# A fused transformer block on one core: norm sums by a product with ones, a later second key group, two y tiles in the weight ring, and last products by token tile

## The chip, the cores and the metric

The kernel runs on one core of a Trainium2 chip. It is one launch. The metric is the device time of that launch in microseconds (us), median of several runs. Five engines work side by side, each on its own queue of instructions: TensorE (PE, matrix products into PSUM banks), VectorE (DVE), ScalarE (ACT), GpSimd (POOL) and SyncE (SP, which issues most DMA transfers). PEld is TensorE's loading of the stationary operand.

## What is computed

A decoder block for 512 tokens of width 2048 in fp32, one sequence: a root-mean-square norm, one wide projection, eight attention heads of kind A (compressed, selected and windowed attention, mixed by gates), sixteen narrow heads of kind B (a band of 128 tokens with a sink), each widened with a SiLU gate, then an output projection, the residual sum and a final norm.

```python
for l in range(DEPTH):
    h = _rmsnorm(x, norm_g[l])
    proj = h @ w_in[l]
    (qa, kca, vca, ksa, vsa, kwa, vwa, za, ga,
     qb, kb, vb, zb) = jnp.split(proj, offsets, axis=-1)
    ...
    o_a = gates[..., 0:1] * o_cmp + gates[..., 1:2] * o_sel + gates[..., 2:3] * o_win
    y_a = o_a.reshape(B, S, WIDTH_A) * jax.nn.silu(za)
    qb = _rope(_heads(qb, N_HEADS_B, HEAD_DIM_B)).reshape(B, S, N_KV_B, GROUP_B, HEAD_DIM_B)
    o_b = _banded_attention(qb, _rope(_heads(kb, N_KV_B, HEAD_DIM_B)), _heads(vb, N_KV_B, HEAD_DIM_B),
                            WIN_B, sink=sinks[l].reshape(N_KV_B, GROUP_B))
    y_b = o_b.reshape(B, S, WIDTH_B) * jax.nn.silu(zb)
    x = x + jnp.concatenate([y_a, y_b], axis=-1) @ w_out[l]
return _rmsnorm(x, final_g)
```

## The kernel before

**Split products.** Each fp32 operand is held as a high half in a rounded fp32 type (ScalarE copies it) and a low half (VectorE subtracts the high half from the original). A product is three matmuls, high by high, high by low, low by high (`mm3`, lines 90 to 92). So each weight that arrives by DMA in a `raw` tile takes a ScalarE pass (`whi`, line 68) and a VectorE pass (`wlo`, line 69), both of 128x1024; `wp` is a ring of three such buffers.

**The norm.** The tokens' squares are summed into `sqa` (128 x 512: tokens along the free axis). Four products with a column of ones (line 159) give the sums with tokens on partitions, `rstd` is one over their root, and four copies and four transposes (165, 166) spread it over the partitions as `rstdb` (167). `cosA` and `sinA` are scaled by `rstdb` (170, 171) before the first rope.

**The projections** use 512 columns a matmul and two PSUM banks, `pj`, that rotate. `q_rope` is three VectorE passes (95 to 97) that read the bank and a GpSimd add (349). A head's attention transposes probabilities (443, 578), splits them (`ph` on ScalarE, 377; `pl` on VectorE, 378), multiplies them with the values (450 to 452, 465, 467) and finishes into a y tile `yp` (364).

**From A to B.** After the last A head, key projection `wkb` is roped into `kb1`, query projection `wz[16]` follows, and `build_kv` makes for each of two key groups a doubled copy `kd` (four VectorE copies, 506), its high half `KBH` (507) and low half `KBL` (508), and then the values' halves `VB`. Eight steps over pairs of B heads follow, each with a projection for the next query and one for its gate `zr` (340).

**The output projection** is split by 512 output columns, n = 0 to 3. For n = 0, eight units of weights of two y tiles each go into four banks (`split_y`, 625 and 626, makes the halves of all 16 y tiles). For n = 1 to 3 the products of pairs are combined with fewer multiplications: y combinations named p, u, q (`combos`, 638 to 641), weights that are sums of quarters, and seven products by name (p, 22, u, 21, w, 12, q) whose banks are then added and subtracted. A sum of weight quarters is made by `summed`: SP loads one quarter, GpSimd issues a DMA that adds another to it (762). `ch` holds a running sum on VectorE (769); `u4` is the weight of product 12 (sum `s2`), `u5` of u, `u6` of q, and `s1` belongs to w. The halves of a weight are made by `split_to` (629, 630).

**The end.** `square` (655) sums squares of a row's columns on ScalarE, `pre_norm` (665) adds them, `final` takes the root and its reciprocal (670, 671), scales four pieces of 512 columns (674 on ScalarE, 676 and 678 on VectorE) and writes each by a DMA of 256 KB (675 on ScalarE's queue, 677 and 679 on SP's). The last products in order are u, 21, w, 12, q, of which only u and q are made token tile by token tile.

**What sets the order.** The program is written in one sequence, but a scheduler of the framework puts each engine's instructions in an order of its own by estimated readiness, and sets the waits. A pool's buffers rotate: a tile waits until the earlier tile in its buffer is no longer read. `issue_after` holds an instruction behind a named one. On each engine, instructions run in the order that results.

Of the kernel before, what the change touches and what calls it, by code (L numbers as in the profile page):

```python
# [10 lines left out]
F32 = mybir.dt.float32  # L11
# [22 lines left out]
def hybrid_block(ctx, tc, xT, xtm, w0, w1s, w2s, wz, wkb, wo0, wos, cw1, cw2, cpos, rope, tabs, sinks, gT, fg, out):  # L34
# [53 lines left out]

    def mm3(ps, ah, al, bh, bl, first, last, go_on=False):
        pe.matmul(ps, ah, bh, start=first, stop=False, skip_group_check=go_on)  # L90
        pe.matmul(ps, ah, bl, start=False, stop=False, skip_group_check=go_on)  # L91
        pe.matmul(ps, al, bh, start=False, stop=last, skip_group_check=go_on)  # L92

    def rope_mul(t1, t2, ps, cos, sin):
        dve.tensor_tensor(out=t1, in0=ps, in1=cos, op=ALU.mult)
        dve.tensor_tensor(out=t2[0:64], in0=ps[64:128], in1=sin[64:128], op=ALU.mult)
        dve.tensor_tensor(out=t2[64:128], in0=ps[0:64], in1=sin[0:64], op=ALU.mult)  # L97
        return t1, t2
# [38 lines left out]
    ones = s0.tile([P, 1], F32, name="ones")  # L137
# [29 lines left out]
    act.activation(rstdb, psr, AF.Copy)  # L167
# [177 lines left out]
    def q_rope(ps, cos, sin):  # L345
        t1 = wk.tile([P, S], F32, name="t1", tag="t1")
# [152 lines left out]
    def build_kv(t1):  # L499
        for g in range(2):  # L500
            kd = wk.tile([P, S], F32, name="kd", tag="t1")
            for half in range(2):
                for v in range(2):
                    d = half * 64 + v * 32
                    r = half * 64 + g * 32
                    dve.tensor_copy(kd[d:d + 32], t1[r:r + 32])
            act.activation(KBH[:, g, :], kd, AF.Copy)
            pool.tensor_tensor(out=KBL[:, g, :], in0=kd, in1=KBH[:, g, :].bitcast(F32), op=ALU.subtract)
# [113 lines left out]
    rs2 = so.tile([P, NQ, 2], F32, name="rs2")  # L622

# [9 lines left out]
    ops = {}  # L633

    def combos(m):
        f1, f2 = 2 * m, 2 * m + 1
        a11, a21, a12, a22 = yt[f1][:, H0], yt[f1][:, H1], yt[f2][:, H0], yt[f2][:, H1]
        dve.tensor_tensor(out=a21, in0=a11, in1=a21, op=ALU.subtract)
        dve.tensor_tensor(out=a11, in0=a11, in1=a12, op=ALU.subtract)
        dve.tensor_tensor(out=a12, in0=a12, in1=a21, op=ALU.subtract)  # L640
        dve.tensor_tensor(out=a22, in0=a22, in1=a12, op=ALU.subtract)
        for nm, src in (("p", a11), ("u", a12), ("q", a21)):
            hi = cmb.tile([P, 256], F32R, name=f"{nm}h{m}")
            lo = cmb.tile([P, 256], F32R, name=f"{nm}l{m}")
# [22 lines left out]
    def final(t, part):  # L667
# [5 lines left out]
        for n in range(2):  # L673
            act.activation(v[n], v[n], AF.Copy, scale=r)
            nc.scalar.dma_start(out[:, t, n * 512:n * 512 + 512], v[n])
        dve.tensor_scalar(v[2], v[2], r, None, op0=ALU.mult)
        nc.sync.dma_start(out[:, t, 1024:1536], v[2])
        dve.scalar_tensor_tensor(out=v[3], in0=v[3], scalar=r, in1=fgt[1][:, 512:1024], op0=ALU.mult, op1=ALU.mult)
# [37 lines left out]
    def halves(raw):  # L716
        hi = wp.tile([P, 1024], F32R, name="whi", tag="whi")
        lo = wp.tile([P, 1024], F32R, name="wlo", tag="wlo")
        split_to(hi, lo, raw)
        return hi, lo  # L720

    fgt = []
    for n in range(1, 4):
        xs.append([late(2 * n - 2 + T) for T in range(2)])
        src = wos[n - 1]
        ba, bb, bx, bc = [b.rearrange("p (t c) -> p t c", c=256) for b in banks(n)]
# [57 lines left out]
        product(ba, [halves(load(raw(), 0, g)) for g in range(2)], "p", True)  # L784
        e3 = scratch()
        act.activation(e3, ba, AF.Copy)
# [38 lines left out]
        else:  # L825
            by = psf1.tile([P, S], F32, name="oa", tag="oa").rearrange("p (t c) -> p t c", c=256)
            bxt = [bx, by]
# [19 lines left out]
            product(bc, [halves(c) for c in s1], "w", True)  # L847
            s2 = summed(raw, 0, 2)
            for t in range(2):
                times_g(2, t)  # L850
            plus(xa[1], xa[1], bc)
            u4 = [halves(c) for c in s2]
            u6 = [halves(c) for c in ch]
            for t in range(2, 4):
                square(ssq[:, t, 4:5], xs[3][1][:, t - 2, :])
                pre_norm(t, 4)
                final(t, ssq[:, t, 4:5])
            product(ba, u4, "12", False)
            plus(xb[0], xb[0], ba, ALU.subtract)
            plus(xa[0], xa[0], ba)  # L860
            for t in range(2):
                square(ssq[:, t, 4:5], xa[0][:, t, :])
                pre_norm(t, 5)
# [78 lines left out]
```

## Time and profile before

| what | us |
|---|---|
| median of three runs (850.31 to 850.93) | 850.83 |
| the profiled execution | 850.5 |
| its span on the core | 848.7 |
| VectorE busy | 597.1 |
| ScalarE busy | 404.7 |
| GpSimd busy | 94.1 |

The page gives each engine's busy time and its share of the span. A timeline row gives start, duration, engine, line, operation, output and input by their names in the program, shape, and in square brackets the idle time of that engine before it and what ended it. A list of waits gives the instruction, what released it, total, number and longest. In this kernel 128x512 matmuls are recorded at about 0.40 us each, but overlap: their starts are nearer to each other than that.

### The profile page before, as it was taken

The page shows a single profiled execution, that of the slowest core. Times are in us where ns is not written, and L with a number is a line of the kernel's source. Part 1 is how long each engine was busy: PE and PEld are TensorE (multiplying, and loading weights), DVE is VectorE, ACT ScalarE, POOL GpSimd, SP SyncE. Part 2 cuts the span into 40 slices and gives each one's busy share as a digit, 9 for nine tenths or more (in the row PEclk, how much of TensorE's full clock was granted, in tenths as well). Part 3 has the DMA queues.
Part 4 walks back from the last instruction along what each step waited for, and adds up shares of the span by engine and source line. Part 5 has one row for each costly group of instructions (what it writes and reads, how often), then busy time and mean ns, then how long its engine had stood idle before and what let it go on. Part 6 is the DMA issues. An engine that isn't in the chain of part 4 may idle for free.

```text
span 848.7 us, 12742 instructions
## 1 busy us (share of the span) xinstructions
PE 833.0 (98%) x4776; PEld 727.2 (86%) x4776; DVE 597.1 (70%) x1244; ACT 404.7 (48%) x845; POOL 94.1 (11%) x71
## 2 busy tenths in 40 slices
PE   9999999999999999999999999999999999999994
PEld 7787899988888888888888788888888788999994
DVE  7829574645676765665767698777677799768785
ACT  6724345443554443544443456444543747444436
POOL 4500002011110110110111210111011000000010
PEclk9999999999999999999999999999999999999998
DMA  9642275542221212121221212221223137895975
GB/s 326 202 128 75 78 228 179 170 124 75 75 75 50 65 60 75 51 75 61 90 75 51 86 64 75 76 90 59 75 75 99 51 85 262 215 292 127 283 176 198
DMA packets 33773, 101.40 MB, mean 119 GB/s; under 512 B 4016, under 2 KB 4016, under 8 KB 33712
## 3 DMA queue, kind: packets, MB, share of 16 engines
q1 hardware_dynamic: 30400, 90.90, 33.0%
q0 software_dynamic: 2016, 7.34, 4.9%
q10 hardware_dynamic: 1296, 2.36, 0.8%
q8 instruction: 37, 0.61, 0.3%
q14 instruction: 24, 0.20, 0.1%
HBM read 96.39 MB, written 4.19 MB: 119 GB/s over the span
## 4 chain that ended last, share of the span: by engine, by line
PE 90%; DMA 3%; DVE 2%; ACT 2%; issue 1%; POOL 0%; ACTq 0%; SPq 0%; DVEq 0%; POOLq 0%
PE pj L91 17%; PE pj L92 17%; PE pj L90 17%; PE oa L90 4%; PE oa L92 4%; PE oa L91 4%; PE bank L92 4%; PE bank L90 4%; PE bank L91 4%; PE sp L408 3%; PE tp L443 2%; DMA xr<-xT 1%; PE tp L578 1%; DMA raw<-wos 1%; PE op L452 1%
## 5 line engine op out<-in xcount | busy, mean ns | idle before, releaser
L90 PE MATMUL pj<-xh,whi 128*128 128x512 f32 x560 | 222.8, 398 | 1.2 <-DVE t L97 1.2
L91 PE MATMUL pj<-xl,whi 128*128 128x512 f32 x560 | 222.2, 397 | 0.0
L92 PE MATMUL pj<-xh,wlo 128*128 128x512 f32 x560 | 221.9, 397 | 0.0
L69 DVE TENSOR_TENSOR wlo<-raw,whi 128x1024 fp32r<-128x1024 f32 (+2 forms) x130 | 149.8, 1158 | 75.1 <-ACT whi L68 71.7
L68 ACT ACTIVATE whi<-raw 128x1024 fp32r<-128x1024 f32 (+2 forms) x129 | 124.9, 971 | 153.0 <-PE pj L91 65.0
L90 PEld LDWEIGHTS pj<-xh,whi 128*128 128x128 f32 x560 | 105.4, 188 | 23.1 <-DVE t L97 1.4
L91 PEld LDWEIGHTS pj<-xl,whi 128*128 128x128 f32 x560 | 105.4, 188 | 22.4 <-issue 1.0
L92 PEld LDWEIGHTS pj<-xh,wlo 128*128 128x128 f32 x560 | 105.4, 188 | 22.4
L349 POOL TENSOR_TENSOR t<-t,t 128x512 f32<-128x512 f32 x17 | 35.9, 2114 | 388.8 <-DVE t L97 370.1
L90 PE MATMUL oa<-whi,yh 128*128 128x256 f32 (+1 forms) x208 | 61.9, 299 | 0.6 <-ACT yh L625 0.6
L91 PE MATMUL oa<-wlo,yh 128*128 128x256 f32 (+1 forms) x208 | 62.2, 299 | 0.0
L92 PE MATMUL oa<-whi,yl 128*128 128x256 f32 (+1 forms) x208 | 61.6, 299 | 0.0
L378 DVE TENSOR_TENSOR pl<-tp,ph 128x512 fp32r<-128x512 f32 x56 | 37.8, 685 | 33.3 <-ACT ph L377 33.2
L377 ACT ACTIVATE ph<-tp 128x512 fp32r<-128x512 f32 x56 | 32.5, 595 | 57.0 <-PE tp L443 44.6
L90 PEld LDWEIGHTS oa<-whi,yh 128*128 128x128 f32 x208 | 39.1, 188 | 2.1 <-ACT yh L625 0.8
L92 PEld LDWEIGHTS oa<-whi,yl 128*128 128x128 f32 x208 | 39.2, 188 | 1.4
L91 PEld LDWEIGHTS oa<-wlo,yh 128*128 128x128 f32 x208 | 39.2, 188 | 1.3
L91 PE MATMUL bank<-wlo,xh 128*128 128x256 f32 (+1 forms) x128 | 40.1, 315 | 0.0
L92 PE MATMUL bank<-whi,xl 128*128 128x256 f32 (+1 forms) x128 | 39.9, 314 | 0.0
L557 ACT ACTIVATE ttb<-ttb,mnb 128x256 f32<-128x256 f32 (+1 forms) x64 | 30.1, 471 | 18.2 <-DVE mnb L550 17.6
L90 PE MATMUL bank<-xh,whi 128*128 128x512 f32 x96 | 37.2, 398 | 0.4 <-ACT whi L68 0.4
L91 PE MATMUL bank<-xl,whi 128*128 128x512 f32 x96 | 37.4, 394 | 0.0
(277 smaller groups left out, 1718.3 us busy)
## 6 DMA issues: line engine op xcount, KB each, us to landing
raw<-wz SPq DMA_DIRECT2D x64, 512.0 KB, 3.7
raw<-cw SPq DMA_DIRECT2D x16, 512.0 KB, 3.7
raw<-wos SPq DMA_DIRECT2D x14, 512.0 KB, 4.6
rw<-wos SPq DMA_DIRECT2D x12, 512.0 KB, 5.0
xr<-xT SPq DMA_DIRECT2D x16, 256.0 KB, 5.3
raw<-w SPq DMA_DIRECT2D x8, 512.0 KB, 4.4
raw<-wo SPq DMA_DIRECT2D x8, 512.0 KB, 3.7
raw<-w SPq DMA_DIRECT2D x15, 256.0 KB, 4.6
```

The source lines that it names most:

```text
L68: act.activation(hi[:, :width], raw[:, :width], AF.Copy)
L69: last["lo"] = dve.tensor_tensor(out=lo[:, :width], in0=raw[:, :width], in1=hi[:, :width].bitcast(F32), op=ALU.subtract).ins
L90: pe.matmul(ps, ah, bh, start=first, stop=False, skip_group_check=go_on)
L91: pe.matmul(ps, ah, bl, start=False, stop=False, skip_group_check=go_on)
L92: pe.matmul(ps, al, bh, start=False, stop=last, skip_group_check=go_on)
L349: pool.tensor_tensor(out=t1, in0=t1, in1=t2, op=ALU.add)
L377: act.activation(ph, tp, AF.Copy)
L378: dve.tensor_tensor(out=pl, in0=tp, in1=ph.bitcast(F32), op=ALU.subtract)
L408: pe.matmul(sp[:, a:b], qq[:, qs], kk[g][:, ko:ko + b - a], start=pi == 0, stop=pi == 2)
L443: pe.transpose(tp[:, e * 256 + i * P:e * 256 + i * P + P], views[2 * i + w][2][:, kt * P:(kt + 1) * P], ident)
L452: pe.matmul(oc, VL[:, kt, w, vs], ph[:, es], start=False, stop=False)
L557: act.activation(tv, tv, AF.Exp, bias=mn[:, e, v:v + 1], scale=-1.0, accum_out=dn[:, e, v:v + 1])
```

## The change

The change has five parts.

1. The norm's sums come from one product of a 128x128 tile of ones with `sqa`, whose result is already spread over the partitions; the root and the reciprocal are taken on 128x512. The column sums for `rstd` stay. Copies and transposes go.
2. `build_kv` becomes `build_k` for one group and `build_v`. The second group is built after the query projection of the next heads. `kd` and `kb1` now lie in the pool `wb`, and the copies are held behind the last rope issued.
3. The halves of y tiles 0 and 1 for the first unit (n = 0) are made in a buffer of the weight ring (`ey`), ahead of the point at which the pool of the y halves opens. `split_y` still makes all y halves.
4. In the last stage (n = 3) the products p, w, 12 and q are made by token tile, each tile in a bank of its own, and sums, squares and `final` follow tile by tile in the order 2, 3, 0, 1. The halves of `s2` go into the buffers of the p combinations, free after product p. All pieces but one of the output leave on SP's queue. `behind` holds a tile's sums behind the previous tile's last scaling.
5. A root of one column is taken at the start of the output projection, so that the table of that function is loaded there.

```diff
-    ones = s0.tile([P, 1], F32, name="ones")
+    ones = s0.tile([P, P], F32, name="ones")
...
     psr = bank(6)
+    pe.matmul(psr, ones, sqa, start=True, stop=True)
+    psc = bank(7)
     for t in range(NQ):
-        pe.matmul(psr[:, t:t + 1], sqa[:, t * P:(t + 1) * P], ones, start=True, stop=True)
-    act.activation(rstd, psr[:, 0:NQ], AF.Sqrt, bias=eps, scale=1.0 / D)
+        pe.matmul(psc[:, t:t + 1], sqa[:, t * P:(t + 1) * P], ones[:, 0:1], start=True, stop=True)
+    act.activation(rstdb, psr, AF.Sqrt, bias=eps, scale=1.0 / D)
+    act.activation(rstd, psc[:, 0:NQ], AF.Sqrt, bias=eps, scale=1.0 / D)
+    dve.reciprocal(rstdb, rstdb)
     dve.reciprocal(rstd, rstd)
-    psr = bank(7)
-    for t in range(NQ):
-        rb = s0b.tile([P, P], F32, name="rb", tag="rb")
-        dve.tensor_copy(rb, rstd[:, t:t + 1].to_broadcast([P, P]))
-        pe.transpose(psr[:, t * P:(t + 1) * P], rb, ident)
-    act.activation(rstdb, psr, AF.Copy)
...
-    def build_kv(t1):
-        for g in range(2):
-            kd = wk.tile([P, S], F32, name="kd", tag="t1")
-            for half in range(2):
-                for v in range(2):
-                    d = half * 64 + v * 32
-                    r = half * 64 + g * 32
+    def build_k(t1, g):
+        kd = wb.tile([P, S], F32, name="kd", tag="kd")
+        for half in range(2):
+            for v in range(2):
+                d = half * 64 + v * 32
+                r = half * 64 + g * 32
+                with tc.issue_after(last["rope"]):
                     dve.tensor_copy(kd[d:d + 32], t1[r:r + 32])
...
-    kb1 = q_rope(proj(wkb), cosB, sinB)
+    kb1 = q_rope(proj(wkb), cosB, sinB, wb.tile([P, S], F32, name="kb1"))
     q2 = qb_evac(proj(wz[16]))
-    build_kv(kb1)
+    build_k(kb1, 0)
+    build_v()
     for i in range(8):
         tts = softmax_b(i, q2)
         if i < 7:
             q2 = qb_evac(proj(wz[17 + i]))
+        if i == 0:
+            build_k(kb1, 1)
         st = z_evac(proj(wz[24 + i]))
         if i == 7:
+            ey = [wp.tile([P, 1024], F32R, name=nm, tag=nm) for nm in ("whi", "wlo")]
+            y01 = ypair[0].rearrange("p a b -> p (a b)")
+            act.activation(ey[0], y01, AF.Copy)
+            dve.tensor_tensor(out=ey[1], in0=y01, in1=ey[0].bitcast(F32), op=ALU.subtract)
...
+    act.activation(rs2[:, 0, 0:1], ssq[:, 0, 0:1], AF.Sqrt)
...
+    pq = [cmb.tile([P, 8, 256], F32R, name=f"p{e}", tag=f"p{e}") for e in "hl"]
...
+    @contextmanager
+    def behind(t):
+        if t == 2:
+            yield
+        else:
+            with tc.issue_after(last["fin_act"]), tc.issue_after(last["fin_dve"]):
+                yield
...
-                mm3(acc[t], yh[f][:, ts], yl[f][:, ts], hi[:, ws], lo[:, ws], f == 0, f == 15)
+                if f < 2:
+                    ah, al = [y[:, f * S:(f + 1) * S] for y in ey]
+                else:
+                    ah, al = yh[f], yl[f]
+                mm3(acc[t], ah[:, ts], al[:, ts], hi[:, ws], lo[:, ws], f == 0, f == 15)
...
-            product(bc, [halves(c) for c in s1], "w", True)
+            u1 = [halves(c) for c in s1]
             s2 = summed(raw, 0, 2)
...
-            u4 = [halves(c) for c in s2]
+            p4 = [cmb.tile([P, 8, 256], F32R, name=f"p{e}", tag=f"p{e}").rearrange("p a b -> p (a b)") for e in "hl"]
+            u4 = [halves(s2[g], [p[:, g * 1024:g * 1024 + 1024] for p in p4]) for g in range(2)]
             u6 = [halves(c) for c in ch]
...
+            for t in range(2):
+                with tc.issue_after(recent["mm"]):
+                    product(bct[t], u1, "w", True, (t,))
+                with behind(2 + t):
+                    plus(xa[1][:, t, :], xa[1][:, t, :], bct[t][:, t, :])
+                    square(ssq[:, 2 + t, 4:5], xs[3][1][:, t, :])
+                final(2 + t, ssq[:, 2 + t, 4:5])
             for t in range(2):
-                product(bxt[t], u6, "q", False, (t,))
-                v = xb[0][:, t, :]
-                plus(v, v, bxt[t][:, t, :])
-                square(ssq[:, t, 5:6], v)
+                with tc.issue_after(recent["mm"]):
+                    product(bat[t], u4, "12", False, (t,))
+                va, vb = xa[0][:, t, :], xb[0][:, t, :]
+                with behind(t):
+                    plus(va, va, bat[t][:, t, :])
+                    plus(vb, vb, bat[t][:, t, :], ALU.subtract)
+                    square(ssq[:, t, 4:5], va)
+                    pre_norm(t, 5)
+                with tc.issue_after(recent["mm"]):
+                    product(bxt[t], u6, "q", False, (t,))
+                plus(vb, vb, bxt[t][:, t, :])
+                square(ssq[:, t, 5:6], vb)
                 final(t, ssq[:, t, 5:6])
```

More of the change, by code (lines that the diff above doesn't have):

```diff
@@ L1 @@
-from contextlib import ExitStack
+from contextlib import ExitStack, contextmanager
 import numpy as np
@@ L91, in mm3 @@
         pe.matmul(ps, ah, bl, start=False, stop=False, skip_group_check=go_on)
-        pe.matmul(ps, al, bh, start=False, stop=last, skip_group_check=go_on)
+        recent["mm"] = pe.matmul(ps, al, bh, start=False, stop=last, skip_group_check=go_on).ins
     def rope_mul(t1, t2, ps, cos, sin):
@@ L96, in rope_mul @@
         dve.tensor_tensor(out=t2[0:64], in0=ps[64:128], in1=sin[64:128], op=ALU.mult)
-        dve.tensor_tensor(out=t2[64:128], in0=ps[0:64], in1=sin[0:64], op=ALU.mult)
+        last["rope"] = dve.tensor_tensor(out=t2[64:128], in0=ps[0:64], in1=sin[0:64], op=ALU.mult).ins
         return t1, t2
@@ L714, in late, with halves, as_pair @@
         return yp.tile([P, 2, S], F32, name=f"late{k}", tag=f"yp{k}")
-    def halves(raw):
-        hi = wp.tile([P, 1024], F32R, name="whi", tag="whi")
-        lo = wp.tile([P, 1024], F32R, name="wlo", tag="wlo")
+    def halves(raw, to=None):
+        hi, lo = to or [wp.tile([P, 1024], F32R, name=nm, tag=nm) for nm in ("whi", "wlo")]
         split_to(hi, lo, raw)
         return hi, lo
+    def as_pair(b):
+        return b.rearrange("p (t c) -> p t c", c=256)
     fgt = []
@@ L725, in hybrid_block @@
         src = wos[n - 1]
-        ba, bb, bx, bc = [b.rearrange("p (t c) -> p t c", c=256) for b in banks(n)]
+        ba, bb, bx, bc = [as_pair(b) for b in banks(n)]
         xa = [x[:, :, H0] for x in xs[n]]
@@ L782, in plus @@
             dve.tensor_tensor(out=out, in0=a, in1=b, op=op)
-        product(ba, [halves(load(raw(), 0, g)) for g in range(2)], "p", True)
+        u3 = [halves(load(raw(), 0, g)) for g in range(2)]
         e3 = scratch()
-        act.activation(e3, ba, AF.Copy)
+        if n < 3:
+            product(ba, u3, "p", True)
+            act.activation(e3, ba, AF.Copy)
+        else:
+            bat = [ba, as_pair(psf1.tile([P, S], F32, name="oa", tag="oa"))]
+            bxt = [bx, as_pair(psf1.tile([P, S], F32, name="oa", tag="oa"))]
+            bct = [bc, as_pair(psp.tile([P, S], F32, name="pj", tag="pj"))]
+            for t in range(2):
+                product(bat[t], u3, "p", True, (t,))
+                act.activation(e3[:, t, :], bat[t][:, t, :], AF.Copy)
         r22 = [load(rw(), 3, g) for g in range(2)]
```

39 lines of the change are left out of this document (18 added, 21 removed).

## The prediction

> **What bounds the kernel now.** I read the page first, then the list of what TensorE waited for, then the last 16 us by stretches, then the timelines of TensorE, ScalarE, VectorE and GpSimd around each edit.
>
> ```profile
> span 848.7 us, 12742 instructions
> PE 833.0 (98%) x4776; PEld 727.2 (86%) x4776; DVE 597.1 (70%) x1244; ACT 404.7 (48%) x845; POOL 94.1 (11%) x71
> ```
> ```profile
> PE pj L90 <- DVE t L97: 1.2, 1, 1.2
> PE bank L92 <- DVE wlo L69: 0.9, 1, 0.9
> ```
> ```profile
> 837.58 0.28 PE L92 MATMUL oa<-whi,ql 128*128 128x256 f32 x1
> ```
> ```profile
> 842.00:844.00 2.00, 0.00 (x0) 0.00 (x0) 0.96 (x2) 1.26 (x2) 0.00 (x0) 0.50 1.02 373
> 846.00:848.70 2.70, 0.00 (x0) 0.00 (x0) 0.00 (x0) 0.00 (x0) 0.00 (x0) 0.50 0.34 127
> ```
>
> TensorE sets the time: 833.0 of 848.7 us busy, and its waits are few (the two longest are shown: us in total, times, longest). So an edit can win only one of those short waits or part of the 848.7 - 837.58 = 11.1 us from the start of the last matmul to the end, in which only output is finished and written (the stretches give engine busy times, then granted clock, DMA share, GB/s). Everything else can only lose: any new wait of TensorE goes straight into the time. I therefore walked along the changed instruction order of each engine and asked, at each place the diff touches, what now stands ahead of an operand TensorE needs.
>
> **Norm sums.**
> ```profile
> 64.08 0.69 DVE L170 TENSOR_TENSOR cosA<-cosA,rstdb 128x512 f32<-128x512 f32 x1 [5.26 <-ACT rstdb L167]
> 70.72 2.36 DVE L69 TENSOR_TENSOR wlo<-raw,whi 128x1024 fp32r<-128x1024 f32 x2
> ```
> ```profile
> 475.88 0.61 PE L467 MATMUL op<-pd,VF 128*128 128x128 f32 x4
> 665.78 0.18 DVE L559 RECIPROCAL dnb<-dnb 128x4 f32<-128x4 f32 x1
> 839.80 0.16 DVE L671 RECIPROCAL rs<-rs 128x1 f32<-128x1 f32 x1 [0.38 <-ACT rs L670]
> ```
> VectorE idled 5.26 us for rstdb, so rstdb's users ran late and the next weight's low half at 70.72 was late: that is the 0.9 us wait. With rstdb made at once the whole queue moves forward and the wait goes: -0.9. TensorE pays an fp32 product of 512 columns: an fp32 product of 128 columns is two records at a pitch of 0.11 us (0.61 for four, the last lasting 0.27), so 0.22, times 4 is 0.88, less four transposes at 0.11 that go: +0.44. The reciprocal of 128x512 is in no row: at least a 128x512 pass (0.69, the L170 row), at most 0.16 plus 511 columns at (0.18 - 0.16) / 3 = 3.6 us; either is less than the 5.26 that VectorE idled, so it costs nothing. Part: -0.5.
>
> **Second key group later.**
> ```profile
> L90 PE MATMUL pj<-xh,whi 128*128 128x512 f32 x32 | 12.8, 399 | 0.0
> ```
> ```profile
> 468.31 0.60 ACT L377 ACTIVATE ph<-tp 128x512 fp32r<-128x512 f32 x1 [0.63 <-PE tp L443]
> ```
> ```profile
> 470.18 0.68 DVE L378 TENSOR_TENSOR pl<-tp,ph 128x512 fp32r<-128x512 f32 x1
> 476.78 0.69 DVE L364 SCALAR_TENSOR_TENSOR yp<-op,st 128x512 f32<-128x512 f32 x1
> 482.81 0.68 DVE L97 TENSOR_TENSOR t<-pj,sinA 64x512 f32<-64x512 f32 x1
> ```
> ```profile
> 483.55 0.51 PE L90 MATMUL pj<-xh,whi 128*128 128x512 f32 x1 [1.24 <-DVE t L97]
> ```
> The 1.24 us wait is a rope queued behind the kd copies; half of the copies move behind it, and the wait goes: -1.2. But the order changes just before. The first row (groups of TensorE from 452 to 478) shows 32 of each kind, some 95 projection matmuls, mixed into the last A head's attention: they fill the time in which its transposes are copied and split. In the changed order of VectorE the rope of kb1, which frees the first of two "pj" banks, stands behind that head's finish (L364), because kb1's buffer and the copies now belong to another pool and another order. Until then the third projection has no bank, and nothing fills. Two bare chains result. First, transposes, ph (0.60), then on VectorE a weight's low half (1.22) ahead of pl (0.68): TensorE has some 1.9 us of its own products for about 4.6 us of it, 2.7 lost (1.5 if the low half is not ahead). Second, after the last op product (0.27): L364 and three rope passes at a pitch of 0.60 to 0.70 and the bank: 0.27 + 0.05 + 2.6 = 2.9. Together 5.5, bounds 4.4 and 5.5, and 0 if the banks come free as before. Part: +4.3.
>
> **y tiles in the weight buffer.**
> ```profile
> 669.50 0.67 DVE L340 TENSOR_TENSOR zr<-pj,rstdb 128x512 f32<-128x512 f32 x1
> 686.57 1.22 DVE L69 TENSOR_TENSOR wlo<-raw,whi 128x1024 fp32r<-128x1024 f32 x1
> ```
> ```profile
> 670.59 0.50 PE L90 MATMUL oa<-whi,yh 128*128 128x512 f32 x1 [0.56 <-ACT yh L625]
> 670.92 0.39 PE L91 MATMUL oa<-wlo,yh 128*128 128x512 f32 x1
> 671.16 0.39 PE L90 MATMUL oa<-whi,yh 128*128 128x512 f32 x1
> ```
> The 0.56 us wait for the first yh goes: -0.6. But a buffer of the weight ring (three deep) is now held by y until the first products are done. In the changed order TensorE has 52 matmuls of 512 columns (pitch 0.23, the last rows), 14 transposes and 12 products of the last B head between the last projection and unit 2's low half: 12.1 + 1.5 + 1.5 = 15.1 us. VectorE's queue from zr to that low half is nearly what it was: 686.57 + 1.22 - 669.50 = 18.3 us. The difference, 3.2, and the 0.4 us from the last projection's end to zr are a stall of 3.6. Before, some 14 more matmuls of the output product stood ahead of it. Bounds: 0 and 4. Part: +3.0.
>
> **Last stage, operands of the last products.**
> ```profile
> 805.58 2.26 ACT L629 ACTIVATE whi<-ch 128x1024 fp32r<-128x1024 f32 x2 [1.26 <-DVE ch L769]
> 827.00 1.06 ACT L629 ACTIVATE whi<-raw 128x1024 fp32r<-128x1024 f32 x1 [5.12 <-DMA raw<-wos]
> 827.96 1.04 ACT L629 ACTIVATE whi<-ch 128x1024 fp32r<-128x1024 f32 x1
> ```
> ```profile
> 806.67 2.42 DVE L630 TENSOR_TENSOR wlo<-ch,whi 128x1024 fp32r<-128x1024 f32 x2
> ```
> ```profile
> 808.34 0.86 POOL L762 DMA_DIRECT2D raw<-wos  x1 [14.87 <-DVE wlo L630]
> 821.29 0.86 POOL L762 DMA_DIRECT2D raw<-wos  x1 [7.97 <-DMA raw<-wos]
> ```
> ```profile
> 809.22 0.40 PE L90 MATMUL oa<-whi,uh 128*128 128x256 f32 x2
> 814.92 0.28 PE L90 MATMUL oa<-whi,yh 128*128 128x256 f32 x1
> ```
> This is the dear one. The split of s2 (the sum for product 12) has buffers of its own now, so nothing but its data holds it, and in the changed order ScalarE takes it right after e3, ahead of both whi<-ch that product u needs; VectorE likewise takes pl<-raw, then e<-e,oa (128x512), ahead of both wlo<-ch. Its data is late: GpSimd issues the accumulating load at 808.34, and the second such load took 827.00 - 821.29 = 5.7 us until ScalarE went on, so the first lands near 814.1. Its issue and its waits are unchanged by the diff, and so are those of the load ahead of it on SP's queue. The 827.00 row shows what a queue does meanwhile: ScalarE stood 5.12 us with whi<-ch, ready, behind it. So: ph 814.1, two whi done by 816.1 (0.97 and 1.06 after), pl until 816.3, e 0.6 (as L378), first wlo until 818.1 (1.21, half of the 806.67 row). Product u, which began at 809.22, gets its low half 8.9 us later; a few matmuls on the high half fit ahead: 8.4. Bounds 6.9 (on whi alone) and 10.1 (both wlo needed). Then u, 21, w follow at 814.92 - 809.22 = 5.7 each; w needs s1, whose second half stands behind s2's second: its buffer comes free with pl at 816.3, and a load and an accumulating load of at most 5.7 each end at 827.7; ph, whi and wlo bring w's halves by 831, while w is due at 818.1 + 2 x 5.7 = 829.5, or 831.4 with the clock below. I take 0, bounds 0 and 4. Part: +8.4.
>
> **Clock.**
> ```profile
> L143 PE MATMUL bank<-still x40: 219/314/314, 1.1 to 5.0; 128*128 128x128 bf16 x40
> ```
> After the last matmul the granted clock is 0.50 (the 842 to 844 stretch), so an idle TensorE loses it; at the start, from 1.1 to 5.0 us, most of 40 equal matmuls take 314 ns and the fastest 219 (the row gives least, median, most), so a cold start lasts most of 3.9 us. If an idle of 8 us costs the clock and half speed lasts about 3.8 us, half of that is lost: +1.9, bounds 0 and 3.9. [...]
>
> **Tail.**
> ```profile
> 838.93 0.42 ACT L655 ACTIVATE sq<-late 128x256 f32<-128x256 f32 x1
> 839.25 0.19 ACT L655 ACTIVATION_READ_ACCUMULATOR sq<-late 128x1 f32 x1
> 839.47 0.29 ACT L670 ACTIVATE rs<-ssq,rs 128x1 f32<-128x1 f32 x1
> ```
> ```profile
> 839.01 0.41 DVE L782 TENSOR_TENSOR late<-late,oa 128x256 f32<-128x256 f32 x1
> 840.00 0.49 DVE L676 TENSOR_SCALAR late<-late,rs 128x512 f32<-128x512 f32 x1
> 840.40 0.75 DVE L678 SCALAR_TENSOR_TENSOR late<-late,rs,late 128x512 f32<-128x512 f32 x1
> ```
> ```profile
> DMA to landing us min/median/max: 2.0/3.7/5.0
> ```
> Before, eight late writes queue at 373 GB/s behind one another. In the changed order tiles 2, 3 and 0 are finished while later products run (5.7 us for 12 and q of one tile against some 3 us of finish), and the square-root table is loaded long before. After the last matmul there is tile 1 alone: 0.3 to its end, add 0.41, square and read 0.61, root 0.29, reciprocal 0.16, L676 and L678 1.15, steps between 0.2: 3.1; then the last write, 2.0 to land on an idle queue, 0.7 more for a neighbour; then about 1.7 to the end of the span (the last stretch is 0.34 x 2.7 = 0.9 us busy, ending near 847.0). 7.5, against 11.1: -3.6, bounds -3.0 and -3.9. Were tile 0's writes still running, 0.7 for each would return.
>
> **Sum.** 850.5 (the profiled execution) - 0.5 + 4.3 + 3.0 + 8.4 + 1.9 - 3.6 = 864.0. The median of the runs, 850.83, is 0.3 above that execution: 864.3.
>
> **Rivals.** (1) Faster: the queues do not hold. If ScalarE and VectorE let ready work pass the late split, or the banks come free as before, the three stalls vanish and only the gains stay: 850.8 - 0.5 - 1.2 - 0.6 - 3.6 = 844.9. It decides once the three stalls cost under 5.9 together. Against it: the 5.12 us row. (2) s2's sum lands before 809, 5 us sooner: u isn't held: 864.3 - 8.4 - 1.9 = 854.0. For it: the load on SP is old by then; against: the diff leaves its waits alone. (3) The clock stays: 862.4. For it: no gap in mid-kernel shows it. (4) s2's second half also holds w, +4: 868.3. For it: the margin above is nil.
>
> **Numbers.** Forecast 0.55, (1) 0.07, (2) 0.10, (3) 0.13, (4) 0.13, and 0.02 that stalls and gains cancel. The range 857 to 869 leaves out (1), (2) and the last, 0.19, and takes in the lower bounds of the key and y parts (864.3 - 1.1 - 3.6 = 859.6, less 1.5 on u and part of the clock). About 0.2% is what a measurement of this kernel can tell from no change; slower by more: 0.91, faster: 0.07, within: 0.02.
>
> **What would show it.** In the changed profile TensorE's list of waits should have one of about 8 us ended by a low or high half of ch at the first product with "uh", with a granted clock under 1 behind it; one of about 3 us ended by a rope of kb1 before B's first attention; 2 to 4 us ended by a low half after the last B head. The wait on L97 with 1.2 and the one of 0.9 should be gone, and the last matmul should start some 7.5 us ahead of the end. If the first wait is missing, the forecast is wrong by 10 us; if all are, rival (1) holds.

## The result and the profile after

The changed kernel takes 869.87 us (median of five runs, 869.74 to 871.89) against 850.83 for the kernel before: ratio 1.023, 95% interval 1.0216 to 1.0245. It is 2.3% slower, 5.6 us above the forecast of 864.3 and 0.9 above the range. The profiled execution is the run of 869.87; its span is 19.4 us longer than before. The page of the changed kernel, span, busy times and granted clock:

```profile
span 868.1 us, 12747 instructions
...
PE 841.5 (97%) x4774; PEld 733.2 (84%) x4774; DVE 604.6 (70%) x1245; ACT 406.4 (47%) x848; POOL 91.8 (11%) x71
...
PEclk9999999999999999999998999999999999999979
```

TensorE runs two instructions fewer and is busy 8.5 us longer: nearly the same work took longer in places. What it waited for, in the changed kernel (us in total, times, longest):

```profile
PE oa L92 <- ACT whi L639: 10.1, 2, 9.0
PE pj L92 <- DVE t L99: 2.8, 1, 2.8
PE oa L93 <- DVE wlo L69: 1.8, 1, 1.8
PE op L451 <- DVE pl L378: 1.2, 2, 0.9
...
PE opb L587 <- DVE pl L378: 0.8, 1, 0.8
```

Line numbers have moved: L90 to L92 are now L92 to L94, L97 is L99, L629 and L630 are L639 and L640, L762 is L792. The first row is the hold of product u, the second and fourth the two bare chains of the key stage, the third and the last the y tiles. The old waits of 1.2 (rope) and 0.9 (low half) are gone. So each stall that the prediction named is there. The hold, in the timelines of ScalarE and VectorE of the changed kernel:

```profile
814.24 0.39 ACT L825 ACTIVATE e<-oa 128x256 f32<-128x256 f32 x1 [0.38 <-PE oa L94]
826.91 1.06 ACT L639 ACTIVATE ph<-raw 128x1024 fp32r<-128x1024 f32 x1 [12.29 <-DMA raw<-wos]
827.87 1.99 ACT L639 ACTIVATE whi<-ch 128x1024 fp32r<-128x1024 f32 x2
```
```profile
828.00 1.23 DVE L640 TENSOR_TENSOR pl<-raw,ph 128x1024 fp32r<-128x1024 f32 x1 [9.40 <-ACT ph L639]
...
829.74 2.35 DVE L640 TENSOR_TENSOR wlo<-ch,whi 128x1024 fp32r<-128x1024 f32 x2
```

ScalarE stands 12.29 us behind the split of `s2` (`ph<-raw`, for product 12, three products later), with both `whi<-ch` of u behind it. TensorE meanwhile:

```profile
819.68 0.29 PE L94 MATMUL oa<-whi,yl 128*128 128x256 f32 x1
828.96 0.79 PE L92 MATMUL oa<-whi,uh 128*128 128x256 f32 x2 [9.00 <-ACT whi L639]
830.86 0.58 PE L92 MATMUL oa<-whi,yh 128*128 128x256 f32 x1 [1.10 <-ACT whi L639]
831.23 0.41 PE L93 MATMUL oa<-wlo,uh 128*128 128x256 f32 x1
831.45 0.41 PE L94 MATMUL oa<-whi,ul 128*128 128x256 f32 x1
...
834.24 0.27 PE L93 MATMUL oa<-wlo,uh 128*128 128x256 f32 x1
834.36 0.28 PE L94 MATMUL oa<-whi,ul 128*128 128x256 f32 x1
```

By starts it idles 9.2 us before u and 1.4 after u's first two matmuls. Then pitches are 0.21 us at first and 0.12 from 834 on. That is the clock. It also falls at the two smaller stalls. Stretches of 3.41 us of the changed kernel, cut where the granted clock changes (TensorE busy and number, granted clock, DMA share, GB/s):

```profile
458.53:461.94 3.41, 1.64 (x10) 1.00 0.02 2
461.94:465.36 3.42, 2.40 (x6) 0.50 0.02 5
465.36:468.77 3.41, 3.41 (x10) 0.50 0.00 0
...
690.64:694.05 3.41, 1.59 (x8) 1.00 0.03 4
694.05:697.46 3.41, 3.41 (x10) 0.50 0.79 225
...
820.34:823.75 3.41, 0.00 (x0) 1.00 0.77 214
823.75:827.17 3.42, 0.00 (x0) 0.50 1.06 210
827.17:830.58 3.41, 0.79 (x2) 0.50 1.01 195
830.58:833.99 3.41, 3.13 (x14) 0.50 0.49 162
```

A stretch with 1.77 or 1.82 us of idle time (3.41 less 1.64 or 1.59) was followed by one at half. After the stretch behind the key wait, 1.0 idle, the clock stayed at half; after stretches with none or 0.3 (the last row) it was full again.

**The balance.** I took the same instruction in both traces and followed its shift: 1.7 us earlier once the projections run steadily, 5.2 later after the key stage (6.9 lost there), 9.7 later at the first u of n = 1 (4.5 lost), 10.6 later at the end of product 22 (0.8 lost), 22.9 later at the last matmul (12.4 lost, nearly all at u), 19.4 at the end of the span: the last matmul now starts 7.6 us before it, not 11.1.

```profile
860.52 0.28 PE L94 MATMUL oa<-whi,ql 128*128 128x256 f32 x1
```

### The profile page after: what moved, and what is told of

Read it like the earlier page. It is cut to its first block, busy times and chain, and to the rows that moved or that the text cites. A ratio compares the mean times of both kernels' runs of the same rounds, so it can differ in the third digit from the quotient of the medians.

```text
span 868.1 us, 12747 instructions
## 1 busy us (share of the span) xinstructions
PE 841.5 (97%) x4774; PEld 733.2 (84%) x4774; DVE 604.6 (70%) x1245; ACT 406.4 (47%) x848; POOL 91.8 (11%) x71
## 4 chain that ended last, share of the span: by engine, by line
PE 89%; DMA 3%; issue 3%; ACT 3%; DVE 3%; POOL 0%; SPq 0%; DVEq 0%; ACTq 0%; POOLq 0%
PE pj L93 16%; PE pj L92 16%; PE pj L94 16%; PE oa L93 4%; PE oa L94 4%; PE oa L92 4%; PE bank L94 4%; PE bank L92 4%; PE bank L93 4%; PE sp L408 3%; DMA xr<-xT 2%; PE tp L443 2%; PE tp L580 1%; PE op L451 1%; PE spb L546 1%
## 5 line engine op out<-in xcount | busy, mean ns | idle before, releaser
L92 PE MATMUL pj<-xh,whi 128*128 128x512 f32 x560 | 223.6, 399 | 2.8 <-DVE t L99 2.8
L94 PE MATMUL pj<-xh,wlo 128*128 128x512 f32 x560 | 222.7, 398 | 0.0
L69 DVE TENSOR_TENSOR wlo<-raw,whi 128x1024 fp32r<-128x1024 f32 (+2 forms) x130 | 152.7, 1180 | 71.1 <-ACT whi L68 68.5
L92 PEld LDWEIGHTS pj<-xh,whi 128*128 128x128 f32 x560 | 106.0, 189 | 25.1 <-DVE t L99 3.0
L94 PEld LDWEIGHTS pj<-xh,wlo 128*128 128x128 f32 x560 | 106.1, 189 | 22.7
L349 POOL TENSOR_TENSOR t<-t,t 128x512 f32<-128x512 f32 x16 | 32.0, 2003 | 364.7 <-DVE t L99 346.1
L93 PE MATMUL oa<-wlo,yh 128*128 128x256 f32 (+1 forms) x180 | 54.5, 303 | 1.8 <-DVE wlo L69 1.8
L92 PE MATMUL oa<-whi,yh 128*128 128x256 f32 (+1 forms) x180 | 54.1, 303 | 1.1 <-ACT whi L639 1.1
L94 PE MATMUL oa<-whi,yl 128*128 128x256 f32 (+1 forms) x180 | 54.4, 303 | 0.0
L94 PE MATMUL bank<-whi,xl 128*128 128x256 f32 (+1 forms) x128 | 39.9, 313 | 0.0
L92 PE MATMUL bank<-xh,whi 128*128 128x512 f32 x96 | 37.2, 398 | 0.0
L92 PE MATMUL bank<-whi,xh 128*128 128x256 f32 (+1 forms) x128 | 36.8, 315 | 0.4 <-ACT whi L68 0.4
L93 PEld LDWEIGHTS oa<-wlo,yh 128*128 128x128 f32 x180 | 34.1, 190 | 3.3 <-DVE wlo L69 2.0
L92 PEld LDWEIGHTS oa<-whi,yh 128*128 128x128 f32 x180 | 34.4, 192 | 2.6 <-ACT whi L639 1.4
```

Source lines behind the costliest of these rows:

```text
L69: last["lo"] = dve.tensor_tensor(out=lo[:, :width], in0=raw[:, :width], in1=hi[:, :width].bitcast(F32), op=ALU.subtract).ins
L94: recent["mm"] = pe.matmul(ps, al, bh, start=False, stop=last, skip_group_check=go_on).ins
```

## The experiments

Each ratio is against runs of the kernel before on the same chip. Edits are to the changed kernel unless said otherwise.

**1. Undo one loss at a time.** `s2_ring` gives the p buffers to q's weight and splits `s2` in the ring, late, as before the change:

```diff
-            u4 = [halves(s2[g], [p[:, g * 1024:g * 1024 + 1024] for p in p4]) for g in range(2)]
-            u6 = [halves(c) for c in ch]
+            u6 = [halves(c, [p[:, g * 1024:g * 1024 + 1024] for p in p4]) for g, c in enumerate(ch)]
...
+            u4 = [halves(c) for c in s2]
```

> The changed kernel with the two owners of buffers exchanged in the last stage: the halves of product q's weight (a sum that is ready early) go into the p buffers, and the halves of s2, product 12's weight, go back into the weight ring, after product w. Theory (ScalarE's and VectorE's queues stood behind the late accumulating load, and the idle then cost the clock): from the first product u on, nothing is held; the 9.0 us wait and the 1.4 us one behind it go, and the 10.2 us at half clock; 12.6 us less than the changed kernel, 857.3 (856 to 859). Rival (the loss comes from products by token tile in more banks, or from transfers, whoever owns the buffers): 867 to 870.

863.62 us (858.75 to 865.27), 1.0135 [1.0103, 1.0167], 4.6 above the range expected. The 9.0 us wait is gone; u starts 7.8 us nearer to its old place. But by starts w now waits 0.4, 0.4 and 1.1 and 12 another 1.2 and 1.1 for weights that land late, and the clock is at half from 845.6 to 849.0. The hold was the late split; about half of what it cost comes back as smaller waits.

`s2_held` keeps the p buffers and holds the split behind u's last halves:

```diff
+            with tc.issue_after(u5_act), tc.issue_after(u5_lo):
+                u4 = [halves(s2[g], [p[:, g * 1024:g * 1024 + 1024] for p in p4]) for g in range(2)]
```

> The changed kernel with its buffers as they are, but the split of s2 is issued behind the last low half of product u's weight on ScalarE and VectorE. Theory (order in the queue is the cause, not the buffer): u runs on time, and the split, which still waits for the same load, now stands ahead of the halves that product 21 needs; the wait moves to 21's first matmul and is shorter by product u's 5.7 us: about 4 to 5 us there, and one or two windows of half clock; 862 to 865. Rival 1 (the p buffers themselves come free late, or the load is late because of them): u's wait stays, 868 to 870. Rival 2 (engines let ready work pass a waiting instruction): no wait at all, 857.

865.85 us, 1.0164 [1.0147, 1.0181], 0.9 above the range expected. The wait moves one product on, as the theory of queues has it, and is 5.7 us where 4 to 5 were expected. TensorE's list and ScalarE's timeline of this kernel:

```profile
PE oa L92 <- ACT whi L639: 5.7, 1, 5.7
```
```profile
819.24 2.25 ACT L639 ACTIVATE whi<-ch 128x1024 fp32r<-128x1024 f32 x2 [2.87 <-DVE ch L799]
828.50 1.06 ACT L639 ACTIVATE ph<-raw 128x1024 fp32r<-128x1024 f32 x1 [7.01 <-DMA raw<-wos]
829.46 1.99 ACT L639 ACTIVATE whi<-raw 128x1024 fp32r<-128x1024 f32 x2
```

Now u's two `whi<-ch` go ahead of it, and product 21's two `whi<-raw` stand behind it.

`s2_last` holds the split behind w's halves, the last that are due before 12:

```diff
+            with tc.issue_after(u1_act), tc.issue_after(u1_lo):
+                u4 = [halves(s2[g], [p[:, g * 1024:g * 1024 + 1024] for p in p4]) for g in range(2)]
```

> The changed kernel with one thing altered: the split of s2 is held behind the last half of w's weight. Theory (order in the queues alone): the waits before u (9.0 and 1.4 us) and the half clock behind them go, the key and y waits stay; 857 to 859.5, the spread from how many windows of half clock follow the key waits. Rival (the load itself is late for the products it feeds, wherever the split stands): a wait of some us at product 12, 861 to 864.

864.31 us, 1.0151 [1.0133, 1.0169]: some 5 above the range expected and near the rival's, though the wait stands at w and not at 12. u and 21 wait for nothing, and w waits 3.0 us for its own second half, which landed at 833.79:

```profile
PE oa L92 <- ACT whi L639: 3.0, 1, 3.0
```

Half clock from 834.7 to 841.6 follows. So behind the queue there is a second limit, the loads themselves (experiment 4).

`kb1_early` puts `kb1` back into its old pool and builds the second key group ahead of the next query projection (one run, two edits, not told apart):

```diff
-    kb1 = q_rope(proj(wkb), cosB, sinB, wb.tile([P, S], F32, name="kb1"))
+    kb1 = q_rope(proj(wkb), cosB, sinB)
...
+        if i == 0:
+            build_k(kb1, 1)
         if i < 7:
             q2 = qb_evac(proj(wz[17 + i]))
-        if i == 0:
-            build_k(kb1, 1)
```

> The changed kernel with kb1 in the ring of rope buffers again, as before the change, and the second key group built ahead of the next query's rope; kd stays in its new pool. Theory (kb1's new buffer lies in memory that the last A head still reads, so its rope, and with it the projection's bank, waits for that head): the four waits of 5.5 us before B's first projection go, and the stretch at half clock behind them (13 matmuls of 512 columns, 0.2 us more each); the wait of 1.2 us for a rope behind the copies returns; 863 (861.5 to 864.5). Rival (the rope stands behind the last head's finish in VectorE's queue for another reason, or the low half ahead of pl is what costs): at most the 3.0 us of the bank go, 866 to 868.

861.24 us, 1.0122 [1.0104, 1.014]. Its list of TensorE's waits:

```profile
PE oa L92 <- ACT whi L639: 9.8, 2, 8.7
PE oa L93 <- DVE wlo L69: 1.8, 1, 1.8
...
PE opb L587 <- DVE pl L378: 0.8, 1, 0.8
```

Neither key wait is left, the clock stays at 1.00 through the stage, and the old rope wait of 1.2 doesn't return. From there on it runs a steady 8.45 us ahead of the changed kernel: the 6.9 lost there, and some 1.7 by which it is ahead of the kernel before in this stage (1.2 of them the rope wait), less the 0.15 by which it came into the stage later. The time is 0.3 us below the range expected. That the rope waits until memory of its buffer has been read isn't shown: in VectorE's order in the changed kernel the rope has no wait of its own, it stands directly behind the finish of the last A head, which waits for TensorE:

```profile
460.21 0.69 DVE L364 SCALAR_TENSOR_TENSOR yp<-op,st 128x512 f32<-128x512 f32 x1 [0.92 <-PE op L467]
460.82 0.68 DVE L97 TENSOR_TENSOR kb<-pj,cosA 128x512 f32<-128x512 f32 x1
```

`y_back` drops `ey`, so that all y halves come from `split_y` again:

```diff
-            act.activation(ey[0], y01, AF.Copy)
-            dve.tensor_tensor(out=ey[1], in0=y01, in1=ey[0].bitcast(F32), op=ALU.subtract)
...
-                if f < 2:
-                    ah, al = [y[:, f * S:(f + 1) * S] for y in ey]
-                else:
-                    ah, al = yh[f], yl[f]
```

> The changed kernel without the halves of y tiles 0 and 1 in the weight ring: the first unit reads the same y halves as the others, as before the change. Theory (the ring's buffer held by y, and the order it brings, leave too few matmuls ahead of unit 2's low half): the waits of 1.06 and 2.09 us and the window at half clock (1.5 us) go, the wait of 0.8 us for the first y half returns; 866 (865 to 867). Rival (VectorE's queue is as full as before, the wait stays): 869 to 870.5.

867.19 us, 1.0183 [1.0168, 1.0198], 0.2 above the range expected. The waits of 1.8 and 0.8 are gone, the old one of 0.6 for `yh` is back, and no half clock follows at 694. In the profiles it runs 4.2 us ahead of the changed kernel from there to n = 1.

**2. The three together, and the norm alone.** `best_a` has the edits of `kb1_early`, `y_back` and `s2_last`.

> The changed kernel with its three losses undone: kb1 in the rope ring and the second key group ahead of the next rope, the first unit of the output projection on the ordinary y halves, and the split of s2 (still in the p buffers) held on ScalarE and VectorE behind the last half of w's weight. What is left of the change is the norm's product with ones and the tail by token tile. Theory (the change's gains are real and hidden under its waits): no wait of TensorE above 1.1 us, no stretch at half clock before the end; before 850.8 less 1.7 at the norm less 3.6 in the tail is 845.5, with up to 1 us for the second half of s2; 845 to 847. Rival (products by token tile in more banks, or 15 writes on one queue, cost what the tail wins): 848 to 851.

851.56 us, 1.0003 [0.9991, 1.0016], a miss by 5 us and 0.6 above the rival's range, though nearly the whole loss is gone. It runs 3.0 us ahead of the kernel before until product w, and loses 6.1 there, up to 1.7 of it to half clock from 824.1 to 827.5. Its list of waits and GpSimd's timeline (L635 and L636 are the L639 and L640 of the changed kernel):

```profile
PE oa L92 <- ACT whi L635: 2.9, 1, 2.9
...
PE oa L93 <- DVE wlo L636: 0.9, 1, 0.9
```
```profile
804.82 0.86 POOL L784 DMA_DIRECT2D raw<-wos  x1 [14.33 <-DVE ch L791]
...
813.92 0.88 POOL L784 DMA_DIRECT2D rw<-wos  x1 [4.44 <-DMA rw<-wos]
```

w's second weight half is late. SP's load of it, issued at 805.16, ran beside the accumulating load of 804.82 and took 8.0 us; only then could its own accumulating load start (813.92, landed 821.21).

`norm_only` is the kernel before with the norm part alone (the first part of the diff).

> The kernel before with the norm's part of the change alone: the product with a tile of ones, root and reciprocal on 128x512. Theory (the wait of 1.1 us for a low half goes and some shorter ones, the fp32 product costs 0.4): the projections run 1.6 us earlier than before, as in the changed kernel, and it lasts to the end: 849.2 (848.9 to 849.6). Rival (later waits take it back, since buffers and loads after it are not earlier): 850.3 to 851.

850.29 us, 0.9987 [0.9977, 0.9998], at the rival's lower bound, not the theory's. The wait of 0.9 and one of two of 0.4 on a high half go, the projections run 1.3 us earlier, and 0.9 of that is left at the last matmul: 0.45 is lost at product 12, whose second half lands only 0.8 us earlier (826.08, before 826.89).

**3. The clock by itself.** `warm_u` adds 76 matmuls between 22 and u, on operands that are there, with an unused result:

```diff
+                for i in range(76):
+                    filler = pe.matmul(spare[:, 0:256], yh[0][:, 0:P], yh[0][:, 0:256], start=True, stop=True).ins
```

> The changed kernel with 76 extra matmuls of 256 columns into a spare bank between product 22 and product u (their result is not used), which fill the time in which u waits. Theory (an idle TensorE loses the clock): the granted clock stays at 1.00 from 810 us to the end of the products, u's first tile takes no longer than in the kernel before apart from its waits, and the time is some 1.8 us less than the changed kernel's, 868 (866.5 to 869). Rival (the slow stretch comes from something else than idleness, or the lost clock costs nothing): 869.5 to 871, with a clock of 0.50 there all the same.

875.81 us, 1.0288 [1.0271, 1.0306], some 7 above the range expected. The clock does as the theory says: 1.00 from 697 to 844, and u's first token tile takes 4.9 us (829.14 to 834.03) instead of 5.9 (828.96 to 834.84), though one wait in it, for its low half, is longer here (1.7 us). But the scheduler chose another order with the filler in it, and on ScalarE the second split of `s2` now stands ahead of the second half for 21 and both for w:

```profile
841.14 1.06 ACT L639 ACTIVATE ph<-raw 128x1024 fp32r<-128x1024 f32 x1 [10.16 <-DMA raw<-wos]
...
843.05 1.99 ACT L639 ACTIVATE whi<-rw 128x1024 fp32r<-128x1024 f32 x2
```

TensorE then waits 3.3 and 1.4 us for the second half of product 21, and the clock is at half from 844.0 to 850.9:

```profile
843.20 0.38 PE L92 MATMUL oa<-whi,yh 128*128 128x256 f32 x1 [3.32 <-ACT whi L639]
844.98 0.58 PE L93 MATMUL oa<-wlo,yh 128*128 128x256 f32 x1 [1.40 <-DVE wlo L640]
```

The same mechanism took more than the clock gave.

**4. Why w's weight is late.** `p_tile` is the kernel before with product p of the last stage made by token tile and nothing else:

```diff
-        product(ba, [halves(load(raw(), 0, g)) for g in range(2)], "p", True)
+        u3 = [halves(load(raw(), 0, g)) for g in range(2)]
...
+            for t in range(2):
+                product(ba, u3, "p", t == 0, (t,))
```

> The kernel before with one thing of the change: product p of the last stage goes token tile by token tile, in the same bank. Theory (by tile, the weight ring's first buffer is read until the second tile's first half, 1.4 us longer, so the next weight is split and added 1.4 us later, the load into its buffer starts later and runs beside the accumulating load, and w's second half comes late): w waits 2 to 4 us, perhaps with a window of half clock; 853 to 856. Rival (the order of a product's tiles moves nothing outside it): 850.3 to 851.3.

853.99 us, 1.0036 [1.0025, 1.0047]. Going by tile, p reads its first weight half until the second tile, so that ring buffer comes free later: a split that waits for it starts at 801.61 (before: 800.89), and SP's loads behind it 0.7 later. One issued at 807.48 now runs beside GpSimd's accumulating load (807.42, which is 0.9 earlier than before, in another place of the order) and takes 8.8 us, the accumulating one 9.0. GpSimd's last load for w follows at 817.03; before, it was at 812.44. TensorE then waits 2.2 us in all for low halves, most of it in w, as expected. GpSimd of `p_tile`, then of the kernel before:

```profile
807.42 0.86 POOL L762 DMA_DIRECT2D raw<-wos  x1 [14.89 <-DVE ch L769]
...
817.03 0.87 POOL L762 DMA_DIRECT2D rw<-wos  x1 [4.56 <-DVE ch L769]
```
```profile
812.44 0.88 POOL L762 DMA_DIRECT2D rw<-wos  x1 [1.21 <-DVE e L782]
```

`best_c` is `best_a` with p's weights in the outer loop and the token tile in the inner one, each tile in its own bank:

```diff
+            for m in range(8):
...
+                for t in range(2):
+                    r = slice(t * P, (t + 1) * P)
+                    ah, al = ops["p", m]
+                    mm3(bat[t][:, t, :], ah[:, r], al[:, r], hi[:, cs], lo[:, cs], m == 0, m == 7)
```

> The version with the three losses undone, and product p with its weights in the outer loop and the two tiles (in their two banks) in the inner one, so that the ring's buffer comes free as early as before the change. Theory: the waits of 3.1 and 1.1 us at w go, or shrink below 1 us, and no window at half clock remains before the end: 846 to 848. Rival (the loads of s1 and s2 collide whatever frees the ring): 850 to 852.

849.46 us (847.54 to 852.21), 0.9982 [0.997, 0.9994]. w's wait shrinks from 2.9 to 0.8, but 12 waits 1.3 and 0.9 for the second half of `s2`; the time lies between the ranges of theory and rival.

`best_d` is `best_c` with the exchange of buffers of `s2_ring` in place of the hold.

> The same with the buffers exchanged instead of an order forced: q's halves in the p buffers, the halves of s2 in the weight ring. Theory (a ring buffer for s2 is free when its data lands, so nothing is lost by it): 846 to 848, as with the forced order. Rival (s2's second half waits for the ring, and 12 waits for it): 848 to 851.

850.64 us, 0.9979 [0.9963, 0.9995], with its median in the rival's range, in two groups of runs (846.5 to 847.6, and 850.3 to 852.0). The profiled one, of the slower group, again has SP's load (805.03) beside the accumulating one (804.87), 8.3 and 8.6 us, and w waits 2.8. Which of the two is issued first is a matter of 0.2 us; that this alone makes the groups wasn't shown, for no run of the faster group was profiled.

**5. Order the loads.** `q_first` is `best_d` with GpSimd's loads for w ahead of those for `s2`, and product q ahead of 12, so that the late `s2` is needed last:

```diff
-            s2 = summed(raw, 0, 2)
+            s2 = summed(raw, 0, 2, last["acc"])
...
+                    if after is not None:
+                        es.enter_context(tc.issue_after(after))
+                    last["acc"] = pool.dma_start(c, src[q2, g], accum_op=ALU.add).ins
...
+            for k, t in (("q", 0), ("q", 1), ("12", 0), ("12", 1)):
```

> The version with q's halves in the p buffers and the weights of product p in the outer loop, and two things more: GpSimd issues the accumulating loads of s1 ahead of those of s2, so that they no longer run beside each other, and product q goes ahead of product 12, so that s2 is needed 5.7 us later. Theory (which of the two sums' loads runs first decides whether w or 12 waits, and q can fill the time): w's second half is there when w needs it, 12 waits for nothing, no window of half clock before the end, the last matmul starts about 834 and the end is 8 us later, one more sum and square than before: 845 to 847, and the runs lie close together. Rival (the loads of the last stage set its time whatever the order): 849 to 851.

846.45 us (845.43 to 847.99), 0.9942 [0.9927, 0.9957]: 0.6% faster than the kernel before, as expected. GpSimd's timeline, then TensorE's waits, of this kernel:

```profile
806.82 0.86 POOL L787 DMA_DIRECT2D rw<-wos  x1 [16.54 <-DMA rw<-wos]
809.17 0.88 POOL L787 DMA_DIRECT2D rw<-wos  x1 [1.49 <-DVE e L807]
809.80 1.15 POOL L787 DMA_DIRECT2D raw<-wos  x1
```
```profile
...
PE oa L92 <- ACT yh L631: 0.6, 1, 0.6
PE bank L92 <- ACT whi L68: 0.4, 1, 0.4
PE oa L93 <- DVE wlo L636: 0.4, 1, 0.4
```

All that is left are waits the kernel before had (one of 1.2 at the start isn't shown), and one of 0.4. The same instruction runs 3.4 us earlier than in the kernel before once the key stage is over (norm and rope) and 2.6 at the last matmul, and the end comes 8.7 us after that, not 11.1. The profile is 5.0 us shorter in all; the prediction gave norm, rope wait and tail 5.3.

## Why the prediction was wrong in size and right in kind

The sum was 864.0 for a profiled execution that took 869.9, 5.9 more. Its terms fell short by 7.1: 4.1 of half clock behind the two smaller waits, 2.2 of gaps at u, and 0.8 that it had no term for; against that the norm brought 1.2 more than forecast. By its steps:

- **Norm sums**, -0.5: -1.7 where the projections run steadily, 0.5 of which the changed kernel already had before the first norm product, so -1.2. A second wait on a high half went too, and VectorE's reciprocal was hidden, at 3.35 us, near the upper bound; the group of the changed kernel:

```profile
L166 DVE RECIPROCAL rstdb<-rstdb 128x512 f32<-128x512 f32 x1 | 3.4, 3354 | 0.8 <-ACT rstdb L164 0.8
```

- **Second key group**, +4.3: 6.9. The new gaps by starts are 0.8, 1.2, 0.5 and 3.0, 5.5 as worked out, and the old wait of 1.2 went. The other 2.6 is clock: 13 matmuls of 512 columns at a pitch of 0.43 instead of 0.23. `kb1_early` shows both parts.
- **y tiles**, +3.0: 4.5. Gaps of 3.4 against 3.6 in the sum, less 0.6; the rest, some 1.5, is clock again (seven matmuls at 0.2 more). `y_back` shows it.
- **Operands of the last products**, +8.4: gaps of 9.2 and 1.4, 10.6, above the upper bound of 10.1. The mechanism held (`s2_ring`, `s2_held`); the sentence that the loads' issue and waits are unchanged did not. SP's and GpSimd's timelines of the changed kernel:

```profile
817.53 1.49 SPq L764 DMA_DIRECT2D rw<-wos  x2
```
```profile
819.37 0.86 POOL L792 DMA_DIRECT2D raw<-wos  x1 [16.06 <-DVE ch L799]
```

  The accumulating load landed at 826.88, 7.5 us after its issue, not 5.7: SP's second `rw` load was issued at 818.67, 0.7 us ahead of it, and landed at 824.89; before, that one was issued 1.6 ahead. The load was also issued 0.4 us ahead of u's due start, before 0.9. From the split's start to u's low half it was 4.3 us (826.91 to 831.23), where the prediction had 4.0: the chain was right, the load late. Product p by token tile, which the sum left unpriced, brings these loads nearer together when it is made alone (`p_tile`); there it costs 2.1 to 4.0 us by the interval. That it does so in the changed kernel wasn't shown apart.
- **Clock**, +1.9, charged after the 8 us idle alone: this is the step that failed. At u it measured 1.8 (12.4 less the gaps), as predicted. But 2.6 and 1.5 came after the waits of 3 and 2 us in the key stage and at the y tiles, which the prediction had itself forecast and to which it gave no clock, without a reason. With these 4.1 the sum is 868.1, inside the range. In the changed kernel's trace the clock changes at 461.94, 468.77, 694.05, 697.46, 823.75, 833.99 and 864.71 us, whole multiples of one length apart (225.28 us is 66 times 3.413). Nor did it take 8 us without work: the clock went after a stretch of 3.41 us with 1.77 us of idle time in the key stage, and after one with 1.82 at the y tiles, behind a gap of 2.1 us.
- **Tail**, -3.6: -3.5.
- **No term**, 0.8: between u of n = 1 and the hold there is no new wait, but the matmuls of 256 columns start 0.1200 us apart, where in the kernel before it is 0.1187. Why stays open (see the last section).
- **Slips in the working**: 2.7 and 2.9 make 5.6, not 5.5; 816.1 is the end of the first `whi<-ch` alone, for in the changed kernel the second ended 2.95 us after the split's start, not 2.0. Neither is why it failed.

Rival (1) had 0.07 and fell with the first row of the waits. Rival (2) fell too: the load came later, not sooner. Rival (3) fell at three places. Rival (4) didn't happen in the changed kernel. In `s2_last` and `best_a` w did wait some 3 us, for its own late load; in `warm_u` the second split of `s2` held product 21.

## What to carry to other kernels

A buffer of its own takes away the wait that kept an instruction in its place: check what then stands ahead on each engine's queue (ScalarE stood 12.29 us here), and when its data lands. Charge half clock behind TensorE's waits of 2 to 3 us too: here the gaps of 3.0 us in the key stage and 2.1 at the y tiles had two stretches of 3.41 us and one behind them, 2.6 and 1.5 us. When a product goes by tile, ask which weight buffer comes free later and which load then starts beside another.

## What was unexpected of the hardware

- The clock went after stretches of 3.41 us with 1.65 us (`y_back`), 1.77 and 1.82 us idle (the changed kernel; idle time by the modelled ends), and stayed after those with 0.96 (the changed kernel) and 1.24 (`norm_only`). In between it did either: it went after 1.52 in `s2_ring` and stayed after 1.5 in `y_back` and 1.52 in `s2_last`. At half speed, stretches with 1.0 us idle (the changed kernel) and 1.1 (`y_back`) didn't restore it, one with 0.3 did (the changed kernel). One stretch at half costs up to half of 3.41, 1.7 us. The runs of `s2_ring` differ by 6.5 us, those of the changed kernel by 2.2; that the place of a wait in its stretch makes this wasn't shown.
- The first accumulating load of 512 KB took 5.7 us in the kernel before and 5.3 in `q_first`, issued 1.6 and 3.3 us after the plain load ahead of it, and 7.5 to 9.0 where a plain one was issued within 0.7 us of it (the changed kernel, `best_a`, `best_d`, `p_tile`); that plain one took 6.2 to 8.8 us, where it takes 4.9 in the kernel before. The distance to the plain load isn't all: in `best_c` it was 2.1 us, the next accumulating load followed after 1.4, and the first took 7.3.
- In the last stages the matmuls of 256 columns start 0.1187 us apart in eight of the profiles and 0.1200 in six (the changed kernel, `s2_ring`, `s2_held`, `s2_last`, `warm_u`, `best_c`), at a granted clock of 1.00 in both. In the changed kernel it is 0.1200 from n = 1 to the hold of u and 0.1187 at full clock behind it. What sets it wasn't shown; over some 620 matmuls it is 0.8 us.
